# A hybrid Hyena and attention layer on one core: an early skip row, a first stage by channel pairs, and zeros multiplied ahead of it

## The chip, the cores and the metric

The kernel runs on one core of a Trainium2 chip. The core has a matmul engine (PE, TensorE), a vector engine (DVE), a scalar engine (ACT), GpSimd (POOL) and a sync engine (SP), each with an instruction queue of its own that is worked off in order. SP, ACT and POOL issue transfers, which share 16 DMA engines. The metric is the device time of one execution in microseconds.

## The reference

One layer of a bidirectional encoder, for 1024 positions of width 1024, all in float32:

```python
h = rms_norm(x, norm_g)
proj = h @ w_in                       # 1024 x 1024 by 1024 x 3328
hy_in, g_h, q, k, v, g_a = split(proj)
u = centred_short_conv(hy_in, conv_w, conv_b)        # 3 taps
hv, hx1, hx2 = split(u)
filt = hyena_filters(...)             # small sine MLP on positions, times a decay
k_f = two_sided_spectrum(filt)        # two orders, 512 channels
z = hx1 * long_conv(hv, k_f[:, 0], hyena_bias[0])    # y + u * bias
z = hx2 * long_conv(z, k_f[:, 1], hyena_bias[1])
y_a = windowed_sink_attention(rope(rms_norm(q)), rope(rms_norm(k)), v, sink)
y = concat(rms_norm(z) * silu(g_h), rms_norm(y_a) * silu(g_a))
out = x + y @ w_out
```

## The kernel before

**Arithmetic.** Large products run on PE in float32r, a rounded form. Each factor is split into a high part and the rest (`h[:, 0]` and `h[:, 1]` for x, `w_hi` and `w_lo` for a weight), and three matmuls are summed: high by high, high by rest, rest by high. ACT writes the high parts (`x_high`, a copy or a product with the norm's gain), DVE the rests (`x_low`, `lo_part`).

**The prelude** (`prelude`) comes first. x lies transposed, in two halves of 512 positions (h = 0 and 1) with 8 channel tiles k each. `load_x` queues on SP the transfers of x, two channel tiles at a time (512 KB), and among them the weights of the first two projection tiles (`raw[0]` in two pieces, `raw[1]` in one). The first two projections over half 0 (n = 0 and 1) are written out by hand as a list of (tile, low part or not, from k, to k); PE starts the second one only after six of the first one's eight channel tiles. Then come half 1 of both (`part(0, 1)`, `part(1, 1)`), the third projection, and between them x's squares and their sums (`x_square`, `x_add`, `x_sum`), from which the norm's factor is made (`rsqrt`, `x_rows`), and the filter's MLP (`next(mlp)`). `tables()` queues the loads of the DFT tables and of the first decay. `in_order` fixes the order of the prelude on each engine as it is written.

**The main part** is woven from two generators (`weave`): the Hyena branch, then attention, on one side; on the other the projections that are left, tile by tile, which fill PE. Behind the prelude the framework's scheduler sets the order on each engine, from the dependences, the priorities (`high_priority`) and its own estimates; so one edit can shift the order far behind it. The Hyena branch goes through eight units (order o, quarter s of the channels). In each, `filter_spectrum` makes the filter's values (`gen`), multiplies them by the decay (`eo`), adds a row of `hyena_bias` to the first row of `eo` (L626, the row `skip`), and transforms `eo` on PE (`dft`); `long_conv` then transforms u (`fw`), multiplies, and goes back (`inv`). The decay `dec` and the row `skip` of a unit are loaded on SP where `filter_spectrum` begins, but for the first decay. Each has one buffer.

**The output weights** (`wo`) are loaded while the last gate projections run: for the first half eight pieces of 256 KB through two buffers (`output_weights`, L1022 to L1029), so that a load waits until DVE has finished with the piece two before it. The first output products (`po`, L1115 to L1117) are filler for attention.

## Time and profile before

| | us |
|---|---|
| median of 3 runs (lowest to highest) | 648.45 (647.7 to 650.78) |
| the profiled execution | 647.31 |
| its span | 645.5 |
| PE busy | 624.0 (97%) |
| DVE busy | 530.9 (82%) |
| ACT busy | 267.2 (41%) |

The span leaves out 1.8 us of the profiled execution's time, and that execution is 1.1 us below the median. Busy time counts an engine as busy while any instruction of it is in flight. The time that PE sat idle is 645.5 - 624.0 = 21.5 us.

### The profile page before, as it was taken

Reading aid. Unit: us, or ns where it says so; the run is one execution under the profiler, and the core shown is the slowest. Engines: PE = TensorE matmul, PEld = TensorE weight load, DVE = VectorE, ACT = ScalarE, POOL = GpSimd, SP = SyncE. Lnnn points to the kernel's source line nnn. Section 1 sums busy time; section 2 is a strip of 40 time slices with the busy share of each in tenths; the row PEclk is TensorE's granted clock in tenths of the full one; section 3 lists DMA queues with packets and bytes.
Section 4 is the critical chain, followed back from the end, with each engine's and each line's share of the span. In section 5 each row is a group of like instructions: output and inputs, shape, how many; then the busy total and the mean of one; then the engine's idle time right before and its main releaser. Section 6 shows DMA issues by size and latency. Waiting matters only on the chain.

```text
span 645.5 us, 10611 instructions
## 1 busy us (share of the span) xinstructions
PE 624.0 (97%) x3958; PEld 552.6 (86%) x3958; DVE 530.9 (82%) x1187; ACT 267.2 (41%) x505; POOL 65.3 (10%) x83
## 2 busy tenths in 40 slices
PE   5999899999999999999999999999989999999997
PEld 4888898988999889899998898778877888889885
DVE  6959379899799997988999979589997888876431
ACT  6756424325541355441432241445463454444210
POOL 0121102112110131220111101100110000000000
PEclk9999999999999999999999999999996999999999
DMA  8956936767852689684287735733642324313321
GB/s 330 288 129 149 289 87 165 188 141 166 243 119 83 179 205 220 155 184 119 64 207 192 195 99 149 219 115 121 204 150 99 113 83 136 133 34 115 100 76 55
DMA packets 46964, 98.37 MB, mean 152 GB/s; under 512 B 6713, under 2 KB 15425, under 8 KB 46657
## 3 DMA queue, kind: packets, MB, share of 16 engines
q1 hardware_dynamic: 32640, 63.79, 29.9%
q0 software_dynamic: 10720, 26.21, 21.3%
q10 hardware_dynamic: 3552, 7.71, 3.3%
q8 instruction: 31, 0.51, 0.3%
q14 instruction: 21, 0.16, 0.1%
HBM read 53.65 MB, written 22.02 MB: 117 GB/s over the span
## 4 chain that ended last, share of the span: by engine, by line
PE 74%; DVE 13%; DMA 6%; issue 4%; ACT 2%; SPq 0%; POOL 0%; ACTq 0%; POOLq 0%; DVEq 0%
PE dft L636 7%; PE proj L255 7%; PE proj L257 7%; PE proj L256 7%; PE pv L991 5%; PE fw L752 4%; PE po L1116 4%; PE po L1117 4%; PE po L1115 4%; PE inv L793 4%; PE qkv L501 3%; PE qkv L500 3%; PE qkv L499 3%; PE smax L931 2%; DMA woraw<-in_w_out 2%
## 5 line engine op out<-in xcount | busy, mean ns | idle before, releaser
L255 PE MATMUL proj<-h,w_hi 128*128 128x512 f32 x304 | 121.8, 401 | 0.0
L257 PE MATMUL proj<-h,w_lo 128*128 128x512 f32 x304 | 120.0, 395 | 0.0
L256 PE MATMUL proj<-h,w_hi 128*128 128x512 f32 x304 | 119.8, 394 | 0.0
L223 POOL DMA_DIRECT2D w_lo<-wraw x48 | 43.1, 927 | 244.1 <-ACT w_lo L222 223.4
L255 PEld LDWEIGHTS proj<-h,w_hi 128*128 128x128 f32 x304 | 57.2, 188 | 11.1 <-issue 0.7
L256 PEld LDWEIGHTS proj<-h,w_hi 128*128 128x128 f32 x304 | 57.2, 188 | 11.1 <-issue 0.7
L257 PEld LDWEIGHTS proj<-h,w_lo 128*128 128x128 f32 x304 | 57.2, 188 | 10.9
L220 ACT CAST w_hi<-wraw 128x512 fp32r<-128x512 f32 x48 | 29.4, 619 | 70.8 <-PE proj L256 49.0
L500 PE MATMUL qkv<-w_lo,h 128*128 128x256 f32 x192 | 54.7, 285 | 0.0
L501 PE MATMUL qkv<-w_hi,h 128*128 128x256 f32 x192 | 54.6, 284 | 0.0
L499 PE MATMUL qkv<-w_hi,h 128*128 128x256 f32 x192 | 54.6, 284 | 0.0
L991 PEld LDWEIGHTS pv<-vv,pf 128*128 128x128 f32 x352 | 46.5, 199 | 3.5 <-issue 1.4
L991 PE MATMUL pv<-vv,pf 128*128 128x66 f32 x352 | 47.1, 278 | 1.4 <-DVE ao L996 1.3
L636 PE MATMUL dft<-eo,d 128*128 128x128 f32 x352 | 45.4, 276 | 1.7 <-DVE eo L626 1.7
L636 PEld LDWEIGHTS dft<-eo,d 128*128 128x128 f32 x352 | 42.6, 192 | 2.5 <-DVE eo L626 1.9
L500 PEld LDWEIGHTS qkv<-w_lo,h 128*128 128x128 f32 x192 | 36.8, 191 | 0.1
L499 PEld LDWEIGHTS qkv<-w_hi,h 128*128 128x128 f32 x192 | 36.7, 191 | 0.1
L501 PEld LDWEIGHTS qkv<-w_hi,h 128*128 128x128 f32 x192 | 36.8, 191 | 0.0
L936 DVE CUSTOM_DVE_ANT_0 mj<-smax,mask 128x384 f32<-128x384 f32 (+1 forms) x64 | 33.2, 519 | 2.2 <-PE smax L931 1.2
L793 PE MATMUL inv<-V,di 128*128 128x128 f32 x256 | 34.3, 275 | 0.0
L977 ACT ACTIVATE pf<-st 128x768 f32<-128x768 f32 (+1 forms) x32 | 24.2, 757 | 22.0 <-DVE st L974 21.1
L222 ACT ACTIVATE w_lo<-wraw 128x512 fp32r<-128x512 f32 x48 | 29.8, 628 | 8.4 <-PE qkv L500 8.3
(215 smaller groups left out, 1437.3 us busy)
## 6 DMA issues: line engine op xcount, KB each, us to landing
wraw<-in_w_in SPq DMA_DIRECT2D x48, 256.0 KB, 3.5
w_lo<-wraw POOLq DMA_DIRECT2D x48, 256.0 KB, 4.5
hy<-hsc ACTq DMA_DIRECT2D x12, 512.0 KB, 3.4
u<-hy SPq DMA_DIRECT2D x12, 512.0 KB, 3.7
hsc<-hs POOLq DMA_DIRECT2D x9, 511.5 KB, 5.5
hsc<-hraw POOLq DMA_DIRECT2D x9, 511.5 KB, 4.6
x<-in_x_t SPq DMA_DIRECT2D x8, 512.0 KB, 7.4
dec<-in_decay SPq DMA_DIRECT2D x8, 512.0 KB, 5.7
```

What stands on the lines that cost most here:

```text
L222: nc.scalar.mul(l, raw, -1.0)
L223: nc.gpsimd.dma_start(l.bitcast(F32), raw, accum_op=ALU.add)
L255: nc.tensor.matmul(pt, hi[:, k], xh, start=k == 0, stop=False)
L256: nc.tensor.matmul(pt, hi[:, k], xl, start=False, stop=False)
L257: i = nc.tensor.matmul(pt, lo[:, k], xh, start=False, stop=k == 7)
L499: nc.tensor.matmul(pt[:, b], hh, hi[:, :, k], start=k == 0, stop=False)
L500: nc.tensor.matmul(pt[:, b], hh, lo[:, :, k], start=False, stop=False)
L501: i = nc.tensor.matmul(pt[:, b], hl, hi[:, :, k], start=False, stop=k == 7)
L636: nc.tensor.matmul(out, m, eo[:, t, e], start=n == 0, stop=n == len(terms) - 1)
L793: nc.tensor.matmul(pt[:, k], self.di[:, t + k, c], v[:, t + k, c], start=c == 0, stop=c == 1)
L936: V.tensor_tensor_reduce(out=junk[:, 0:nk], in0=pm[:, 0:nk], in1=mask, op0=ALU.add, op1=ALU.max, scale=1.0, scalar=NEG, accum_out=mx[:, 4 ...
L991: nc.tensor.matmul(pv[:, h], probs[:, n, cols], self.vv[:, k0 + n, g], start=n == 0, stop=n == nk - 1)
```

## The change

Four edits go together.

1. **First stage by pairs.** The list written by hand gives way to a loop: for each pair of x's channel tiles, both projections' high parts, then both projections' low parts. Both weights are loaded in halves, the first halves behind x's first pair, the second halves behind x's third pair, and the order of the work on ACT and DVE follows. Over half 1, `part(0, 1)` and `part(1, 1)` advance in turn, two channel tiles at a time.
2. **Zeros.** A corner of the tile `row`, 128x128, is set to zero, and PE multiplies it by itself 18 times (`WARM`) into a spare bank ahead of the first projection.
3. **First skip row.** It is loaded in `tables()`, behind the first decay (`skip0`).
4. **Later skip rows and decays.** Both loads get the priority of u's loads (`2 * HP`), and the skip row moves to the pool of the decay.

```diff
--- before.py
+++ after.py
@@ -40,6 +40,8 @@
 
 FIRST = 3
 HP = 200
+
+WARM = 18
 RT = math.sqrt(0.5)
 TWO_PI_A = 6.28125
 TWO_PI_B = 2.0 * math.pi - 6.28125
@@ -120,6 +122,8 @@
         nc, a = self.nc, self.a
         pk = cp.tile([P, 192], F32, name="consts")
         nc.scalar.dma_start(pk, a["consts"])
+        self.row = cp.tile([P, 2, 512], F32, name="row")
+        nc.vector.memset(self.row[:, 0, 0:P], 0.0)
         self.ones = cp.tile([P, 1], F32, name="ones")
         nc.vector.memset(self.ones, 1.0)
         nc.scalar.activation(self.ones, self.ones, AF.Sin)
@@ -130,7 +134,6 @@
         self.identr = cp.tile([P, P], F32R, name="identr")
 
         self.rstd = cp.tile([P, 8], F32, name="rstd")
-        self.row = cp.tile([P, 2, 512], F32, name="row")
         self.zssq = cp.tile([P, 4, 8], F32, name="zssq")
 
 
@@ -142,10 +145,9 @@
         for h in range(2):
             for k in range(0, 8, 2):
                 q.dma_start(self.xt[h][:, k : k + 2], a["x_t"][h][:, k : k + 2])
-                if h == 0 and k < 4:
-                    q.dma_start(raw[0][:, 2 * k : 2 * k + 4], a["w_in"][ct[0]][:, 2 * k : 2 * k + 4])
-            if h == 0:
-                q.dma_start(raw[1], a["w_in"][ct[1]])
+                if h == 0 and k in (0, 4):
+                    for n in range(2):
+                        q.dma_start(raw[n][:, k : k + 4], a["w_in"][ct[n]][:, k : k + 4])
         return self.weight_load(ct[2])
 
     def x_high(self, h, k, e):
@@ -291,22 +293,26 @@
         del self.order[:2]
         w = [self.first_slot() for _ in range(2)]
 
+        idle = ps.tile([P, P], F32, tag="g", name=self.nm("idle"))
+        for _ in range(WARM):
+            nc.tensor.matmul(idle, self.row[:, 0, 0:P], self.row[:, 0, 0:P], start=True, stop=True)
+
+
         def lo_part(n, c):
             hi, lo = (x[:, 0, c] for x in w[n])
             V.tensor_tensor(out=lo, in0=raw[n][:, c], in1=hi.bitcast(F32), op=ALU.subtract)
 
         for k in range(0, 8, 2):
             self.x_high(0, k, A)
-            if k < 4:
-                half = slice(2 * k, 2 * k + 4)
-                A.copy(w[0][0][:, 0, half], raw[0][:, half])
             self.x_high(0, k + 1, V if k in (0, 4) else A)
+            if k in (0, 4):
+                for n in range(2):
+                    A.copy(w[n][0][:, 0, k : k + 4], raw[n][:, k : k + 4])
             self.x_low(0, k)
             self.x_low(0, k + 1)
-            if k < 4:
-                lo_part(0, half)
-        A.copy(w[1][0][:, 0], raw[1])
-        lo_part(1, slice(0, 8))
+            if k in (0, 4):
+                for n in range(2):
+                    lo_part(n, slice(k, k + 4))
         raws = [sp.tile([P, S], F32, tag=t, name=self.nm("hraw")) for t in ("raw", "raw", "t2")]
         banks = {}
 
@@ -336,12 +342,11 @@
                 nc.tensor.matmul(banks[n, 0], hi, xh, start=k == 0, stop=False)
                 nc.tensor.matmul(banks[n, 0], hi, xl, start=False, stop=False)
 
-        for n, low, k0, k1 in (
-            (0, 0, 0, 2), (0, 1, 0, 2), (0, 0, 2, 4), (0, 1, 2, 4), (0, 0, 4, 6), (0, 1, 4, 6), (1, 0, 0, 4),
-            (0, 0, 6, 8), (0, 1, 6, 8), (1, 0, 4, 8), (1, 1, 0, 8),
-        ):
-            for k in range(k0, k1):
-                first(n, k, low)
+        for k in range(0, 8, 2):
+            for low in range(2):
+                for n in range(2):
+                    for i in range(k, k + 2):
+                        first(n, i, low)
 
         for k in range(0, 8, 2):
             self.x_high(1, k, A)
@@ -354,12 +359,16 @@
             self.x_square(1, k)
             self.x_add(0, (k + 2) % 8)
         tables()
-        all_of(part(0, 1))
-        next(mlp)
+        c0, c1 = part(0, 1), part(1, 1)
+        for n in range(4):
+            next(c0), next(c1)
+            if n == 1:
+                next(mlp)
         for k in (2, 4, 6, 0):
             self.x_add(1, k)
         next(mlp)
-        all_of(part(1, 1))
+        all_of(c0)
+        all_of(c1)
         self.ahead.append(self.weights(*self.order.pop(0)))
         ss = ps.tile([P, 8, 2], F32, tag="g", name=self.nm("xss"))
         self.x_sum(0, ss)
@@ -601,13 +610,13 @@
         nc = self.nc
         V = nc.vector
         ADD, SUB = ALU.add, ALU.subtract
-        if (o, s) == (0, 0):
-            dec = self.dec0
-        else:
+        dec, skip = self.dec0, self.skip0
+        if (o, s) != (0, 0):
             dec = self.dp.tile([P, 8, CH], F32, tag="dec", name=self.nm("dec"), bufs=1)
-            nc.sync.dma_start(dec, self.a["decay"][s])
-        skip = fp.tile([1, CH], F32, tag="skip", name=self.nm("skip"), bufs=1)
-        nc.sync.dma_start(skip, self.a["hyena_bias"][0:1, o, s * CH : (s + 1) * CH])
+            skip = self.dp.tile([1, CH], F32, tag="skip", name=self.nm("skip"), bufs=1)
+            with self.tc.high_priority(2 * HP):
+                nc.sync.dma_start(dec, self.a["decay"][s])
+                nc.sync.dma_start(skip, self.a["hyena_bias"][0:1, o, s * CH : (s + 1) * CH])
         eo = fp.tile([P, 8, 2, CH], F32, tag="eo", name=self.nm("eo"), bufs=1)
         wf = self.wf[:, o, s].rearrange("p e c -> p (e c)")
         for t in range(0, 8, 2):
@@ -1217,6 +1226,7 @@
                     xp = pool(py, "x", 1, side="right")
                     self.dp = dpool
                     self.dec0 = dpool.tile([P, 8, CH], F32, tag="dec", name="dec0")
+                    self.skip0 = dpool.tile([1, CH], F32, tag="skip", name="skip0")
                     mlp = self.filter_mlp(mp, keep, ps)
                     w0, w1 = (self.filter_weights(o, fw, keep, ps) for o in range(2))
                     start = len(nc.cur_bb.bb.instructions)
@@ -1228,6 +1238,7 @@
                     def tables():
                         nc.sync.dma_start(self.d, a["dft"])
                         nc.sync.dma_start(self.dec0, a["decay"][0])
+                        nc.sync.dma_start(self.skip0, a["hyena_bias"][0:1, 0, 0:CH])
                         nc.sync.dma_start(self.dn, a["dft_neg"])
                         next(w0)
```

The start of PE's queue, before and then after. `proj_188` and `proj_212` are the first projection's bank, `proj_189` and `proj_213` the second's; `idle` is the spare bank.

```order
L336 MATMUL proj_188<-h_89,w_hi 128x512
L337 MATMUL proj_188<-h_89,w_hi 128x512
L336 MATMUL proj_188<-h_89,w_hi 128x512
L337 MATMUL proj_188<-h_89,w_hi 128x512
L334 MATMUL proj_188<-h_89,w_lo 128x512 x2
L336 MATMUL proj_188<-h_89,w_hi 128x512
L337 MATMUL proj_188<-h_89,w_hi 128x512
L336 MATMUL proj_188<-h_89,w_hi 128x512
L337 MATMUL proj_188<-h_89,w_hi 128x512
L334 MATMUL proj_188<-h_89,w_lo 128x512 x2
L336 MATMUL proj_188<-h_89,w_hi 128x512
```

```order
L298 MATMUL idle_166<-row 128x128 x18
L342 MATMUL proj_212<-h_89,w_hi 128x512
L343 MATMUL proj_212<-h_89,w_hi 128x512
L342 MATMUL proj_212<-h_89,w_hi 128x512
L343 MATMUL proj_212<-h_89,w_hi 128x512
L342 MATMUL proj_213<-h_89,w_hi 128x512
L343 MATMUL proj_213<-h_89,w_hi 128x512
L342 MATMUL proj_213<-h_89,w_hi 128x512
L343 MATMUL proj_213<-h_89,w_hi 128x512
L340 MATMUL proj_212<-h_89,w_lo 128x512 x2
L340 MATMUL proj_213<-h_89,w_lo 128x512 x2
```

The zeros stand ahead, and the second projection joins at the first pair of channel tiles rather than behind the sixth tile.

SP's queue around the Hyena branch's first unit: first before, from the loads of u's first tiles on; then after, the prelude's tables and the loads around those of u.

```order
L808 DMA u_606<-hy_63 128x1024
L808 DMA u_736<-hy_67 128x1024
L818 DMA di<-in_dft_inv 128x2048
L610 DMA skip_524<-in_hyena_bias 1x128
L608 DMA dec_781<-in_decay 128x1024
L207 DMA wraw_1487<-in_w_in 128x512
L610 DMA skip_783<-in_hyena_bias 1x128
L808 DMA u_919<-hy_71 128x1024
```

```order
L556 DMA mlp_in<-in_mlp_in 128x904
L1239 DMA d<-in_dft 128x2048
L1240 DMA dec_128<-in_decay 128x1024
L1241 DMA skip_129<-in_hyena_bias 1x128
L1242 DMA dn<-in_dft_neg 128x768
L599 DMA w_13_300<-in_filt_w 64x1024
```

```order
L209 DMA wraw_1510<-in_w_in 128x512
L817 DMA u_629<-hy_63 128x1024
L817 DMA u_759<-hy_67 128x1024
L618 DMA dec_804<-in_decay 128x1024
L619 DMA skip_805<-in_hyena_bias 1x128
L827 DMA di<-in_dft_inv 128x2048
L817 DMA u_942<-hy_71 128x1024
```

The first skip row has gone up to the prelude, ahead of `dn`; behind the loads of u come the second unit's decay and skip row, and the table `di` has gone behind both.

PE's queue where the output products begin, before and then after. `po` is an output bank, `st` the attention scores of a pair of heads, `pv` its values, `bT` transposed queries, `proj` the last projection.

```order
L256 MATMUL proj_4729<-h_90,w_hi 128x512
L257 MATMUL proj_4729<-h_90,w_lo 128x512
L991 MATMUL pv_4746<-vv,pf_4684 128x66
L951 MATMUL bT_4691<-identr,qq_4080 66x128 x4
L951 MATMUL bT_4698<-identr,qq_4080 66x128 x4
L991 MATMUL pv_4746<-vv,pf_4684 128x66 x5
L1115 MATMUL po_4983<-wo_4443,yh 128x512
L1116 MATMUL po_4983<-wo_4443,yh 128x512
L1117 MATMUL po_4983<-wo_4443,yl 128x512
L969 MATMUL st_4736<-qb_4696,kt_3918 128x256
L968 MATMUL st_4736<-qa_4586,kt_3917 128x256
L969 MATMUL st_4736<-qb_4696,kt_3918 128x256
```

```order
L977 MATMUL st_4872<-qa_4616,kt_3940 128x256
L978 MATMUL st_4872<-qb_4726,kt_3941 128x256
L977 MATMUL st_4872<-qa_4616,kt_3940 128x256
L978 MATMUL st_4872<-qb_4726,kt_3941 128x256
L977 MATMUL st_4872<-qa_4616,kt_3940 128x256
L978 MATMUL st_4872<-qb_4726,kt_3941 128x256
L258 MATMUL proj_4752<-h_90,w_hi 128x512
L259 MATMUL proj_4752<-h_90,w_lo 128x512
L1124 MATMUL po_5006<-wo_4466,yh 128x512
L1125 MATMUL po_5006<-wo_4466,yh 128x512
L1126 MATMUL po_5006<-wo_4466,yl 128x512
L1124 MATMUL po_5006<-wo_4466,yh 128x512
```

Before, 20 of attention's matmuls `st` from `qb` stand ahead of the first `po`, and the last projection is finished well ahead of it; after, 29 stand ahead of it and the last projection ends right in front of it.

## The prediction

> **What bounds the kernel now.** I read the page's busy times first, then a table of stretches, then the order of time at the places that the change touches.

> ```profile
> span 645.5 us, 10611 instructions
> PE 624.0 (97%) x3958; PEld 552.6 (86%) x3958; DVE 530.9 (82%) x1187; ACT 267.2 (41%) x505; POOL 65.3 (10%) x83
> ```

> PE is in use for 624.0 of 645.5 us. A change can gain only what PE sits idle, 21.5 us, and what PE runs slowly. The stretches, with the busy time and the count of each engine (first column: length):

> ```profile
> core 0: us, PE busy (x) PEld busy (x) DVE busy (x) ACT busy (x) POOL busy (x), PEclk, DMA share, GB/s
> 0.00:6.96 6.96, 0.00 (x0) 0.00 (x0) 1.20 (x5) 2.92 (x5) 1.16 (x5) 1.00 0.68 219
> 6.96:12.68 5.72, 5.72 (x14) 4.49 (x15) 5.33 (x10) 4.53 (x7) 0.00 (x0) 1.00 1.03 416
> 12.68:20.49 7.81, 7.81 (x36) 6.44 (x35) 7.81 (x13) 7.58 (x11) 0.00 (x0) 1.00 1.04 415
> 68.70:78.30 9.60, 7.86 (x67) 7.66 (x65) 1.60 (x4) 3.13 (x5) 1.75 (x2) 1.00 0.97 317
> 480.00:500.00 20.00, 16.66 (x80) 14.05 (x80) 15.52 (x43) 7.09 (x14) 0.54 (x1) 0.74 0.41 139
> ```

> Three places stand out: 6.96 us before the first matmul, then 14 matmuls in 5.72 us where the next 36 take 7.81; 1.74 us of PE idle at 68.7 to 78.3; and a stretch near 484 us with a low clock. The start in order of time:

> ```profile
> 6.96 0.79 PE L336 MATMUL proj<-h,w_hi 128*128 128x512 f32 x1 [6.96 <-ACT w_hi L302]
> 10.54 0.63 PE L336 MATMUL proj<-h,w_hi 128*128 128x512 f32 x1
> 13.89 0.39 PE L336 MATMUL proj<-h,w_hi 128*128 128x512 f32 x1
> 18.90 1.98 PE L334 MATMUL proj<-h,w_lo 128*128 128x512 f32 x8
> 20.71 0.39 PE L255 MATMUL proj<-h,w_hi 128*128 128x512 f32 x1
> ```

> A matmul of the same shape takes 0.63 us at 10.54 and 0.39 at 13.89, and by the table 14 of them begin in 5.72 us and 36 in the next 7.81, with no wait between: PE starts at about half speed and changes near 12.7 us, after 5.7 us of work. (The column PEclk shows 1.00 there; the spacing decides.) The eight low products, 18.90 to 20.71, show the full pace: 0.226 us each.

> **The change part by part.**

> *Zeros.* They need only the cleared tile. DVE's first instruction now starts at 0.82 us, so I take 1.1 us for PE's first zero product. The nearest rows for the price are the same 128x128 float32 product, eight of them as 16 records, up to the next matmul:

> ```profile
> 0.82 0.06 DVE L124 MEMSET ones<- 128x1 f32 x1 [0.82 <-PEq L1473]
> ...
> 39.29 1.95 PE L187 MATMUL xr<-consts,rsy 128*128 128x128 f32 x16
> 40.99 0.47 PE L255 MATMUL proj<-h,w_hi 128*128 128x512 f32 x1
> ```

> 1.70 / 8 = 0.2125 us each at the full pace, 0.425 at half. If 5.7 us of work bring the clock here too, it is there at 6.8 us: 5.7 / 0.425 = 13.4 zeros slow, 4.6 x 0.2125 = 1.0 us quick, end at 7.8. The first projections then start 0.8 us later than now, but 48 x 0.226 = 10.9 us later they are done: 18.7 in place of 20.5, 1.8 us gained. Bounds: if zeros don't bring the clock at all, they end at 1.1 + 7.65 = 8.75, 14 real matmuls are slow (5.7 us), 34 quick (7.7 us), end at 22.15, a loss of 1.65. If the clock comes early enough that zeros end by 6.96, the gain is 2.65.

> *By pairs.* PE needs a pair every 12 x 0.226 = 2.7 us: at 7.8, 10.5, 13.2 and 15.9. The transfers run at 415 GB/s by the table, so what stands ahead of x's second and third pair, 256 KB more, costs 0.6 us, and ahead of the fourth, 512 KB more, 1.3 us. Rows on ACT that waited for these pairs:

> ```profile
> 7.56 0.72 ACT L157 ACTIVATE h<-x,consts 128x512 fp32r<-128x512 f32 x1 [0.65 <-DMA x<-in_x_t]
> 10.79 1.34 ACT L157 ACTIVATE h<-x,consts 128x512 fp32r<-128x512 f32 x2 [0.56 <-DMA x<-in_x_t]
> ```

> So the second pair is there at 8.2 and the fourth at 12.1, against 10.5 and 15.9: over 2 us each for ACT (0.7 us a tile) and DVE. No wait; half 1 comes as before, since the bytes ahead of it are the same. DVE's work is the same but for four low parts of 512 columns, 4 x 0.69, in place of 2 x 0.69 + 1.22: 0.15 us more.

> *What is late next.* The sums of squares on PE need DVE's additions:

> ```profile
> 21.84 4.54 DVE L173 TENSOR_TENSOR x<-x 128x1024 f32<-128x1024 f32 x4
> 26.37 4.60 DVE L173 TENSOR_TENSOR x<-x 128x1024 f32<-128x1024 f32 x4
> 32.48 1.84 PE L177 MATMUL xss<-ones,x 128*128 128x1 f32 x16
> ```

> DVE works without a pause there and is done at 30.97, with the 0.15 us and a little more about 31.2. PE would come at 32.48 - 1.8 = 30.7 and waits until 31.2. Of 1.8 us, 1.25 are left; even the 2.65 would be cut to that. I take 1.25, and -1.65 to 1.5 as bounds. The two projections over half 1, in turn, need each pair of half 1 later than before, so nothing new waits there; reordering them costs no work.

> *First skip row.* The chain of waits holds a transfer here, and the table of waits shows what it cost PE:

> ```profile
> 68.72 9.15 DMA skip<-in_hyena_bias
> ```

> ```profile
> PE dft L636 <- DVE eo L626: 1.7, 1, 1.7
> ```

> The order of time on DVE, and on SP's queue:

> ```profile
> 67.35 2.48 DVE L620 TENSOR_TENSOR eo<-gen,dec 128x512 f32<-128x512 f32 x4
> 69.75 0.27 DVE L625 TENSOR_TENSOR eo<-eo 1x128 f32<-1x128 f32 x1
> 77.96 0.28 DVE L626 SCALAR_TENSOR_TENSOR eo<-eo,skip 1x128 f32<-1x128 f32 x1 [7.95 <-DMA skip<-in_hyena_bias]
> ```

> ```profile
> 67.34 0.81 SPq L808 DMA_DIRECT2D u<-hy  x2
> 68.20 0.46 SPq L818 DMA_DIRECT2D di<-in_dft_inv  x1
> 68.72 0.46 SPq L610 DMA_DIRECT2D skip<-in_hyena_bias  x1
> ```

> 512 bytes took 9.15 us, behind 2 MB of u and `di`; DVE sat 7.95 us, PE only 1.74, because 64 matmuls of `qkv` stood in between. With the row loaded in the prelude, at about 14 us, it is there long before. The gain is PE's 1.74 us at most, not DVE's eight. Nothing else takes its place by the rows: in the new order 11 `qkv` matmuls, 0.12 us each, lie between the last `gen` and the first `dft`, 1.3 us, while DVE needs about 1.1 us after that `gen` (69.83 - 68.7) and 0.3 for the skip row. Bounds 0 (another wait of the same length) and 1.74; I take 1.7. The extra load in the prelude is one issue of 0.33 us on SP ahead of `dn`, whose first reader is `dft`, 50 us later: nothing.

> *Later rows and decays raised.* No other wait for them is in the trace, so there is nothing to gain directly. They go up in SP's queue and wait there for their one buffer, as a skip row did once already; SP holds what is behind them meanwhile. The second row is the first reader of `di`:

> ```profile
> SPq L610 <- DVE eo L626: 14.1, 1, 14.1
> ```

> ```profile
> 116.87 0.91 PE inv L793 x8
> ```

> Behind the second unit's pair come `di`, u, a store and then weights. In the first unit DVE frees both buffers by about 70 us (69.75 + 0.27), over 40 us before `di` is read. I take zero. The wait of 14.1 us cost PE nothing in the trace; as the outer bound I keep a loss of 1.7 us, a stop like that of the first skip row, if one of the seven pairs reaches a weight tile.

> *What the shift does later.* The Hyena branch now runs up to eight microseconds ahead of the projections that fill PE. PE is at 100% up to 400 us, so nothing shows there. It shows near the first output products, here on PE, ACT and DVE in order of time and as a stretch:

> ```profile
> 481.51 0.50 PE L1115 MATMUL po<-wo,yh 128*128 128x512 f32 x1 [0.87 <-ACT wo L1028]
> 482.22 0.39 PE L968 MATMUL st<-qa,kt 128*128 128x256 f32 x1 [0.21 <-ACT pf L977]
> 484.84 0.80 PE L1115 MATMUL po<-wo,yh 128*128 128x512 f32 x1 [1.64 <-ACT wo L1028]
> ```

> ```profile
> 484.17 0.62 ACT L1028 CAST wo<-woraw 128x512 fp32r<-128x512 f32 x1 [2.00 <-DMA woraw<-in_w_out]
> 487.02 0.62 ACT L1028 CAST wo<-woraw 128x512 fp32r<-128x512 f32 x1 [1.52 <-DMA woraw<-in_w_out]
> ```

> ```profile
> 489.06 0.82 DVE L882 TENSOR_TENSOR qkv<-qkv,rm 128x640 f32<-128x640 f32 x1
> ```

> ```profile
> 484.00:494.00 10.00, 9.16 (x36) 8.28 (x37) 7.58 (x18) 3.34 (x7) 0.25 (x1) 0.50 0.14 52
> ```

> PE waits 0.87 + 0.21 + 1.64 = 2.7 us within 5 us for pieces of the output weights, and then runs at half clock (0.50) for most of ten microseconds; I count 9.2 us, the busy time, half of which is 4.6 us more. Whole price 7.3 us. The new order begins `po` three attention units later against the pieces (29 `st` from `qb` ahead of it, not 20), which helps; but `kT` and `aT` of block 4 now stand between the `po`, and these need DVE's rotation, which was done only at 489.9. I take no difference, and keep 7.3 us either way as the bounds.

> The sum against the execution's own time: 647.3 - 1.25 - 1.7 = 644.35. The median of the runs is 1.1 us above that execution, so 645.4.

> **The rivals.**

> *The cold stretch goes.* Everything above and, near 484 us, no half clock: 4.6 us less, of which DVE's rotation lets PE use perhaps 3 to 4, so 645.4 - 4 = 641.5. For it speaks that six of eight pieces are cast ahead of `po` (three before); against it the new place of `kT`. [...]

> *The start gains nothing.* Zeros don't count for the clock, or PE waits again behind the sums: -1.65 to 0 at the start, 1.7 from the skip row. 645.4 + 1.25 + 1.0 = about 648, no change. Against it: the clock rose at 12.7 us with nothing but work having gone before.

> *Slower: a second cold stretch.* The shifted order near 484 us makes PE wait both for the last pieces of `wo` and, after it, for `kT` of block 4. From the point where the waits in 5 us reach again some 2.7 us, a second 7.3 us is due: 645.4 + 7.3 = 652.7. For it: DVE has both the rotation and the low parts of `wo` queued there. Against it: one longer wait by itself left the clock alone, this one at about 415 us:

> ```profile
> PE kT L908 <- ACT kt L909: 1.4, 1, 1.4
> ```

> **How the numbers follow.** The forecast 645.4 has 0.42, the stretch that goes 0.28, no gain at the start 0.17, a second stretch 0.13. 0.5% of 648.45 is 3.2 us, about what a measurement of this kernel can tell from no change; its bounds are 645.2 and 651.7. The forecast lies on the first bound, a bit under half of it faster (0.19); with 0.28 that is 0.47. The rest of it (0.23) and most of the third case (0.15) are the same: 0.38. The second stretch and a rest of the third case: 0.15. The range reaches down to the second case with its full 7.3 us less a little, 639, and up to 651.5, which leaves out most of the last case. The forecast's own range is 643.5 to 647.5.

> **What the changed profile would show.** Matmul starts 0.23 us apart from the first projection on, the first one at 7 to 8.5 us, the low products of the stage done at about 18.7. PE waiting half a microsecond before the sums. L635 (the skip row's addition) without a wait for a DMA and the first `dft` near 70 us. Near 480 us, waits of PE for `wo` or `kT` and the clock behind them. Wrong would be: spacing of 0.43 us after the zeros; a new wait of PE for `w_hi` between 85 and 400 us, which would mean that SP was held up; two stretches of low clock.

## The result, and the profile after

The changed kernel takes 652.47 us (median of 7 runs, 650.86 to 654.77) against 648.45: a ratio of 1.0061, 95% interval 1.0036 to 1.0086. It is slower by 4 us, where 3 us of gain were forecast. Its profiled execution took 652.58 us, 1.8 of them outside the span, as before. Of the runs further down, one slow execution of `start_alone` (1241.51 us) and one of `before_order_start_alone` (653.39) are left out of the ratios but not of the medians, and without the first the median of `start_alone` is 654.46.

The page of the changed kernel, its span, PE's busy time and PE's granted clock in 40 slices:

```profile
span 650.8 us, 10698 instructions
...
PE 630.2 (97%) x3994; PEld 557.6 (86%) x3994; DVE 532.3 (82%) x1189; ACT 268.3 (41%) x506; POOL 65.4 (10%) x83
...
PEclk9999999998999999989999999999998999999999
```

and the granted clock before:

```profile
PEclk9999999999999999999999999999996999999999
```

PE is busy for 6.2 us more, and 6.1 of these are the zeros, which stand where it sat idle. So its idle time should have fallen to about 15 us; it is 650.8 - 630.2 = 20.6. And the clock dips at three places, in slices 10, 18 and 31; before, at one, in slice 31.

The start, PE in order of time, the sums of squares, and the first transposes behind the prelude:

```profile
1.06 6.08 PE L298 MATMUL idle<-row 128*128 128x128 f32 x36 [1.06 <-DVE ones L128]
18.72 0.39 PE L257 MATMUL proj<-h,w_hi 128*128 128x512 f32 x1
30.49 1.84 PE L179 MATMUL xss<-ones,x 128*128 128x1 f32 x16
51.02 1.13 PE L434 MATMUL uT<-consts,hsc 128*128 128x128 f32 x8
```

The next projection begins at 18.72, against 20.71 before: 2.0 us gained. At the sums (32.48 before) all of it is still there. The first transposes come 1.5 us sooner (52.55 before), but here PE has two more projection products behind it by then (161 since 18.72, against 159 since 20.71; 0.45 us), so nothing of the 2.0 is lost. The first skip row no longer keeps DVE or PE (its addition, the first transform, and the next wait of PE):

```profile
67.89 0.27 DVE L635 SCALAR_TENSOR_TENSOR eo<-eo,skip 1x128 f32<-1x128 f32 x1
68.52 2.39 PE L645 MATMUL dft<-eo,d 128*128 128x128 f32 x20
75.56 1.13 PE L761 MATMUL fw<-u,d 128*128 128x128 f32 x8 [0.63 <-DMA u<-hy]
```

So by 80 us the kernel was some 3 us ahead (2.0 and 1.74 - 0.63 = 1.1), where 1.25 + 1.7 were forecast: the sum came out because the two terms were off in opposite ways, which is luck. Then PE's waits, summed (total, times, longest):

```profile
PE uT L434 <- DMA hsc<-hraw: 8.9, 2, 5.4
PE smax L940 <- DVE mx L945: 3.1, 5, 1.2
```

and the same transposes before:

```profile
PE uT L425 <- DMA hsc<-hraw: 0.3, 1, 0.3
```

`smax` waited 3.7 us in all, with one wait for `den`; before, 0.6. The stretches around the two waits (length, PE, its weight loads, DVE, ACT and POOL busy, granted clock, DMA share, GB/s):

```profile
141.40:144.80 3.40, 1.26 (x6) 0.72 (x4) 3.40 (x6) 2.31 (x2) 1.78 (x2) 1.00 0.77 130
144.80:148.20 3.40, 0.14 (x1) 0.17 (x2) 3.40 (x10) 0.00 (x0) 0.00 (x0) 0.50 1.04 237
148.20:151.60 3.40, 3.40 (x13) 3.01 (x14) 0.10 (x1) 1.07 (x2) 0.00 (x0) 0.50 0.75 177
277.90:281.30 3.40, 0.02 (x1) 0.05 (x1) 3.15 (x10) 2.95 (x4) 1.84 (x3) 1.00 1.03 189
281.30:284.70 3.40, 3.40 (x16) 3.40 (x17) 0.16 (x1) 0.00 (x0) 0.77 (x1) 0.50 1.08 196
```

PE stops at 142.7, the clock halves at 144.8, and when the data land PE works another 3.4 us at half pace; at 277.7 likewise. A third stretch (499.8 to 506.6) follows the waits of `smax`. In the working part of the three, 13 us, half is lost: 6.5 us, against 4.6 before. The account, by waits and clock: -2.0 (start), -1.1 (skip row, 1.74 less the new 0.63), +8.6 (transposes), +1.9 (half clock); near the first output products -2.7 (`wo`, gone), +3.1 (`smax`), -1.9 (`kT`), -1.3 (`pv`). That is +4.6 of the 5.3 us by which the spans differ.

**Why the transposes wait.** The short convolution of a Hyena tile (`short_conv`) goes through four engines behind the tile's last projection: DVE scales the second half into `hraw` (L270), ACT makes the middle tap `hsc` (L412) and the side taps (L422, L423), and POOL adds these to `hsc` by two transfers in series (L425). Then PE transposes (`uT`, L434). This is tile s = 1 of the second projection, the changed kernel, all engines in order of time, from the last product of its projection on:

```profile
124.36 0.39 PE L259 MATMUL proj<-h,w_lo 128*128 128x512 f32 x1
...
131.91 0.69 DVE L270 TENSOR_TENSOR hraw<-proj,row 128x512 f32<-128x512 f32 x1
...
133.26 1.24 ACT L412 ACTIVATE hsc<-hraw,consts 128x1024 f32<-128x1024 f32 x1
...
135.90 0.86 POOL L425 DMA_DIRECT2D hsc<-hs  x1 [8.96 <-ACT hs L422]
...
142.27 0.39 PE L257 MATMUL proj<-h,w_hi 128*128 128x512 f32 x1
142.48 0.86 POOL L425 DMA_DIRECT2D hsc<-hraw  x1 [3.11 <-DVE ism L790]
...
148.06 1.94 PE L434 MATMUL uT<-consts,hsc 128*128 128x128 f32 x8 [5.40 <-DMA hsc<-hraw]
```

and the same tile before:

```profile
111.85 0.39 PE L257 MATMUL proj<-h,w_lo 128*128 128x512 f32 x1
...
118.97 0.68 DVE L268 TENSOR_TENSOR hraw<-proj,row 128x512 f32<-128x512 f32 x1
...
126.78 0.86 POOL L416 DMA_DIRECT2D hsc<-hs  x1 [11.94 <-ACT hs L413]
...
133.78 0.86 POOL L416 DMA_DIRECT2D hsc<-hraw  x1 [6.14 <-DMA hsc<-hs]
...
143.93 1.04 PE L425 MATMUL uT<-consts,hsc 128*128 128x128 f32 x8
```

From `hraw` to the transposes it takes 15.5 us after (131.91 + 0.69 to 148.06), 12.2 of them for the two transfers in series (135.90 to 142.48 to 148.06). (The page puts POOL's wait at 142.48 down to DVE. The first transfer was over no sooner than that result: ACT, which waits for it too, goes on at 141.79.) DVE came to `hraw` 7 us after PE had finished with the tile, being at Hyena work, but it did so before as well (112.1 to 118.97). Nor was the chain as a whole shorter before: from 112.1 to about 138.4 (133.78 and the 4.6 us that the page gives as the median of such a transfer), 26 us; after, from 124.6 to 148.06, 23.5 us. What changed is PE's row. Between a tile's last projection product and its first transpose stand (products counted in the built order; us from the two traces, with the wait of the tile's own transposes taken off):

| | before | changed |
|---|---|---|
| second projection, s = 1 | 148: 72 `proj`, 16 `inv`, 16 `gen`, 28 `dft`, 16 `fw`; 31.9 us | 79, all `proj`; 18.1 us, waits 5.40 |
| third projection, s = 1 | 88; 18.8 us, waits 0.3 | 156; 34.9 us |
| first projection, s = 3 | 148; 31.5 us | 80: 72 `proj`, 8 `uT`; 17.4 us, waits 3.55 |
| the six others, least | 148; 32.0 us | 148; 32.1 us |

The planner put the Hyena branch's transforms ahead of the tile's last product, or behind its transposes, and not between. PE works in order, so the distance in its row is the time that the taps get: 18.1 and 17.4 us, where 23.5 and 21.0 were needed. How much is needed differs from tile to tile and run to run: 18.8 us fell short by 0.3 us before and by 1.5 in before_order_skip_row_alone (below), 19.2 by 3.9 in start_alone.

### The profile page after: what moved, and what is told of

Read it like the earlier page. It is cut to its first block, busy times and chain, and to the rows that moved or that the text cites. A ratio compares the mean times of both kernels' runs of the same rounds, so it can differ in the third digit from the quotient of the medians.

```text
span 650.8 us, 10698 instructions
## 1 busy us (share of the span) xinstructions
PE 630.2 (97%) x3994; PEld 557.6 (86%) x3994; DVE 532.3 (82%) x1189; ACT 268.3 (41%) x506; POOL 65.4 (10%) x83
## 4 chain that ended last, share of the span: by engine, by line
PE 73%; issue 11%; DMA 8%; DVE 6%; ACT 2%; POOL 1%; ACTq 0%; POOLq 0%
PE proj L258 8%; PE proj L259 8%; PE proj L257 8%; PE dft L645 5%; PE pv L1000 5%; PE po L1124 4%; PE po L1126 4%; PE po L1125 4%; PE inv L802 4%; PE fw L761 3%; PE qkv L508 2%; PE qkv L510 2%; PE qkv L509 2%; PE st L977 2%; PE st L978 2%
## 5 line engine op out<-in xcount | busy, mean ns | idle before, releaser
L258 PEld LDWEIGHTS proj<-h,w_hi 128*128 128x128 f32 x304 | 57.5, 189 | 10.9 <-issue 0.7
L1000 PEld LDWEIGHTS pv<-vv,pf 128*128 128x128 f32 x352 | 45.0, 191 | 1.2
L1000 PE MATMUL pv<-vv,pf 128*128 128x66 f32 x352 | 45.0, 269 | 0.0
L802 PE MATMUL inv<-V,di 128*128 128x128 f32 x256 | 35.8, 279 | 0.0
L802 PEld LDWEIGHTS inv<-V,di 128*128 128x128 f32 x256 | 33.4, 196 | 0.8 <-issue 0.2
```

The costliest lines, as they stand in the source:

```text
L258: nc.tensor.matmul(pt, hi[:, k], xl, start=False, stop=False)
L802: nc.tensor.matmul(pt[:, k], self.di[:, t + k, c], v[:, t + k, c], start=c == 0, stop=c == 1)
L1000: nc.tensor.matmul(pv[:, h], probs[:, n, cols], self.vv[:, k0 + n, g], start=n == 0, stop=n == nk - 1)
```

## The experiments

Behind the prelude the written program is the same before and after (4833 instructions, and the one load of the first skip row). So the order itself can be carried over. A table of numbers (`PINNED`) names each engine's instructions in the wanted row, and each is made to follow the one ahead of it, without a semaphore:

```diff
-        Kernel(tc, aps, out).run()
+        k = Kernel(tc, aps, out); k.run(); pin(k)
...
+        for a, b in zip(row, row[1:]):
+            k.tc.add_manual_dep(b, a.name, k.NOSYNC, reason="pinned")
```

Held in its own order in this way, a kernel is the same program as without the table. All times, with the ratio to the kernel before on the same chip (its medians there: 649.0 to 649.8), the profiled span, the transposes' wait for their taps and the time at half clock ahead of the last outputs (by the record of the granted clock):

| run | median us | ratio, 95% | span | `uT` waits | half clock |
|---|---|---|---|---|---|
| before | 648.45 | | 645.5 | 0.3 | 10.2 |
| changed | 652.47 | 1.0061 (1.0036 to 1.0086) | 650.8 | 8.9 | 17.1 |
| after_in_befores_order | 640.57 | 0.9877 (0.9853 to 0.9901) | 637.3 | 0 | 0 |
| before_in_afters_order | 653.44 | 1.0069 (1.0047 to 1.009) | 654.7 | 8.0 | 13.7 |
| start_alone | 655.94 | 1.0111 (1.0082 to 1.014) | 652.7 | 3.9 | 13.7 |
| skip_rows_alone | 648.25 | 0.9993 (0.9978 to 1.0007) | 647.2 | 5.5 | 10.2 |
| transposes_later | 644.96 | 0.9945 (0.9927 to 0.9964) | 643.0 | 0 | 3.4 |
| changed_transposes_one_half_later | 639.53 | 0.9861 (0.9829 to 0.9894) | 637.0 | 0 | 3.4 |
| before_order_skip_row_alone | 645.61 | 0.9961 (0.9934 to 0.9988) | 643.4 | 1.5 | 10.2 |
| before_order_start_alone | 645.46 | 0.9947 (0.9921 to 0.9974) | 642.3 | 0 | 6.8 |
| before_transposes_one_half_later | 652.67 | 1.0058 (1.0039 to 1.0077) | 650.7 | 0.2 | 20.5 |
| repaired_without_zeros | 640.53 | 0.9862 (0.9843 to 0.9882) | 639.1 | 0 | 3.4 |
| repaired_without_pairs | 641.06 | 0.9883 (0.9863 to 0.9904) | 637.2 | 0 | 0 |
| waits_filled_with_zeros | 648.44 | 0.9985 (0.9968 to 1.0001) | 647.2 | 0 (filled) | 6.8 |

**The orders crossed.** First the changed kernel in the order of the kernel before:

> The changed kernel with every engine's instructions behind the prelude held in the order that they had in the kernel before (a table of numbers; only the first skip row's load is gone from it, and the later loads stand where they stood before, so their raising is undone). Theory 'order' (the early edits gain what was forecast, and the loss is the new order behind the prelude, in which the transposes of the short convolution wait for its taps): 647.3 - 1.5 to 1.8 - 1.7 = 644 us (643 to 645.5), transposes waiting 0.5 us or less, one stretch of half clock near 484. Rival 'ahead' (work that comes 3 us earlier collides with transfers whatever its order): 651 to 653, with the waits of the changed kernel or others in their place. Rival 'start lost' (zeros and pairs gain nothing in the end): 646 to 648.

Then the start of the kernel before in the order of the changed one:

> The reverse: the first stage of the kernel before (no zeros, by whole tiles, the two late projections one after the other), with the first skip row in the prelude, and behind the prelude every engine in the order of the changed kernel. Theory 'order': the waits of the transposes are there again (about 9 us in all or a little less, as everything around them moves by the same 1.5 us) with two or three stretches of half clock, 652.5 + 1.5 to 1.8 = 654 us (652.5 to 656). Rival 'ahead': the start is late again, so no collision, 646 to 648.5. Rival 'start lost': 652.5.

The first was 8 us faster than before, more than any theory said; the second is as slow as the changed kernel. Same order, nearly the same waits: the loss belongs to the order behind the prelude (SP's row, with the raised loads, is part of it), not to the edits of the start and the first skip row. The first one's granted clock on its page, its wait for the pieces of `wo`, and the stretch in which the cold clock had been:

```profile
PEclk9999999999999999999999999999999999999999
```

```profile
PE po L1124 <- ACT wo L1037: 1.6, 2, 0.8
```

```profile
480.00:500.00 20.00, 18.27 (x113) 15.21 (x114) 17.82 (x55) 8.75 (x20) 0.00 (x0) 1.00 0.43 139
```

The Hyena branch and attention come 2.5 us (at 141 us) to 4 us (at 480) sooner, PE's waits for the pieces of `wo` shrink to 0.8 us apiece, six microseconds apart, and the clock holds (1.00 where it was 0.74): the 4.6 us of the old cold stretch and 1.1 us of its waits go too. Of the start's 2.0 us a wait of 0.9 for the filter's MLP takes part here: 1.1 + 1.7 + 4.6 + 1.1 = 8.5, measured 8.2 between the spans. This is the profiled execution, one of the two fastest of six (639.06 us, mean granted clock 1.0). In the other four the clock averaged 0.991 to 0.995, at 640.5 to 643.2 us, so it still dipped somewhere; and one of 17 executions of the kernel before kept it (1.0, 645.47 us). The cold stretch is thus a matter of odds, and its whole 4.6 us are not in the medians. In the second, against the 2 or 3 stretches expected, four came.

**Each half of the change by itself, ordered by the planner.** The edits of the start, the changed kernel without those of the skip rows and decays:

```diff
-        dec, skip = self.dec0, self.skip0
-        if (o, s) != (0, 0):
+        if (o, s) == (0, 0):
+            dec = self.dec0
+        else:
 ...
-            with self.tc.high_priority(2 * HP):
 ...
-                        nc.sync.dma_start(self.skip0, a["hyena_bias"][0:1, 0, 0:CH])
```

> Zeros, pairs and the two late projections in turn, without the edits of the skip rows and decays; the order behind the prelude is the planner's own. Theory 'order': 647.3 - 1.5 = 645.8 if its order lets the transposes wait no more than before, and each 1 us of their wait with the half clock behind it comes on top (a reshuffle like the changed kernel's gives 652 to 654). Rival 'raised loads do it': 645 to 646 with no such wait, since nothing is raised. Rival 'start lost': 647 to 648.5.

and the other half, the same lines put into the kernel before (signs turned round):

> The first skip row in the prelude and the later rows and decays raised, on the first stage of the kernel before. Theory 'order': 647.3 - 1.7 = 645.6 if its order keeps the transposes' wait at 0.3 us, 650 to 653 if it is reshuffled like the changed kernel's. Rival 'raised loads do it': 651 to 655 with waits behind a load that SP holds. Rival 'no gain from the row': 647 to 648.5.

Each gets an order of its own with new waits for the taps, so neither half is to blame by itself, and the raised loads are not needed for the loss: nothing is raised in the slowest of all, which is above the 652 to 654 that were expected for a reshuffle. The other half took 648.25 us, between the two figures of 'order' and in the range of the rival 'no gain from the row'; but in its trace the first `dft` no longer waits, and 5.5 us of waits for the taps have come. start_alone also shows what the first skip row can cost (PE waiting for it, and the stretch behind):

```profile
78.08 4.29 PE L645 MATMUL dft<-eo,d 128*128 128x128 f32 x20 [5.23 <-DVE eo L635]
```

```profile
75.00:82.00 7.00, 3.92 (x19) 3.92 (x20) 1.04 (x3) 0.58 (x1) 0.86 (x1) 0.51 1.04 355
```

5.23 us, where before it was 1.74, with the half clock behind it.

**The two waits alone.** Only PE's row is touched:

```diff
 MATMUL proj_1810<-h_90,w_hi 128x512
-MATMUL uT_1615<-consts,hsc_1502 128x128 x4
-MATMUL uT_1620<-consts,hsc_1502 128x128 x4
 ...
 MATMUL inv_967<-V_948,di 128x128
+MATMUL uT_1615<-consts,hsc_1502 128x128 x4
+MATMUL uT_1620<-consts,hsc_1502 128x128 x4
```

> The changed kernel in its own order, held by a table, with one thing moved on PE: the two groups of eight transposes that waited for their taps (at 148 and 281 us) stand 36 and 24 matmuls later. All other engines keep their rows. Theory 'order' in its narrow form (these two waits and the half clock that begins in them are the loss): both waits go, 8.9 us, and two of the three stretches of half clock, about 1.75 us each as PE worked some 3.5 us in each; 652.6 - 8.9 - 3.5 = 640 us (639 to 643, if the inverse products that now come first wait a little for DVE). The third stretch near 500 us stays or moves. Rival 'other places': Hyena work behind the transposes was late too, so another wait takes their place, 648 to 652.

Both waits and both half-clock stretches are gone, by moving 16 transposes. But 7.5 us came of the 12.4 expected. PE's next waits say where the rest is:

```profile
145.72 0.91 PE L802 MATMUL inv<-V,di 128*128 128x128 f32 x6 [0.61 <-DVE V L734]
160.69 1.38 PE L645 MATMUL dft<-eo,d 128*128 128x128 f32 x10 [1.69 <-ACT fc L670]
164.54 1.76 PE L761 MATMUL fw<-u,d 128*128 128x128 f32 x11 [0.93 <-ACT fc L670]
```

The Hyena work behind the transposes was short of DVE and ACT results by 3.2 us here (0.44 more at 275 us): part of what the rival 'other places' said.

**A repair that leaves the order to the planner.** The transposes are released half a projection later:

```diff
-LATE = 0
+LATE = 1
```

> The changed kernel with LATE = 1: the transposes are released behind the second half of the next tile, not the first, and the planner orders everything anew. In its order the least PE work between a tile's last projection and its transposes is 27 us, against 17.9 in the changed kernel. Theory 'order': no wait of the transposes, 652.6 - 8.9 - 3.5 = 640 (639 to 644; the stretch near 500 may come or go with 3 us). Rival 'other places': 648 to 652, since what reads the transposed tiles now comes later and the Hyena branch waits for u.

639.5, as forecast and the lowest median of all (its interval overlaps that of the crossed order). No wait of the transposes is left; the page and the largest wait:

```profile
span 637.0 us, 10699 instructions
...
PEclk9999999999999999999999999999998999999999
```

```profile
PE st L977 <- ACT pf L986: 1.5, 2, 1.1
```

The same number in the kernel before:

> The kernel before with LATE = 1 alone, ordered anew by the planner; least PE work between a tile's last projection and its transposes 23 us (before 18.9). Its transposes hardly waited (0.3 us), so by the theory 'order' there is little to gain: 647.3, less up to 4.6 if the cold stretch near 484 goes, plus up to 3.5 for new waits: 643 to 651. The rival, that the later transposes themselves are the whole gain of the repaired kernel (639.5) and the edits of the start and the skip row give nothing: 639 to 641.

It is 3.8 us slower than before by the ratio, a little above the range expected. The transposes wait 0.2 us, but the first `dft` now waits 3.97 us for the skip row, and the clock is at half for 6.8 us behind it and for 13.7 us near 490. So the later transposes are not a gain by themselves; with the edits they free 13 us.

**The halves in the order of the kernel before.** Both pinned by its table; the skip row without the raising, which the table undoes:

```diff
+                        nc.sync.dma_start(self.skip0, a["hyena_bias"][0:1, 0, 0:CH])
 ...
-        if (o, s) == (0, 0):
-            dec = self.dec0
-        else:
+        dec, skip = self.dec0, self.skip0
+        if (o, s) != (0, 0):
 ...
```

> The kernel before, in its own order on every engine, with one edit: the first skip row's load stands in the prelude. If the edits' gains add up: 647.3 - 1.7 = 645.6, with the cold stretch near 484 as before; if being 1.7 us ahead is enough to end that stretch, 641. 647 to 649 if the row's gain is given back later.

> The kernel before, in its own order behind the prelude, with the edits of the start alone (zeros, pairs, late projections in turn). The first skip row still stands behind u and di on SP, whose issue does not come earlier than their buffers allow, so PE, 1.5 us ahead, should wait 1.5 us longer for it: 647.3 - 0 = 646 to 648. If the gain stands: 645.8, or 641 if the cold stretch near 484 ends too.

By ratio the row brings 0.39%, the start 0.53%, both together 1.23%: about additive within the intervals. By the spans 2.1 and 3.2 us. The row's term was about right (1.7), and the old cold stretch stayed, as expected at 1.7 us ahead. Of the start I expected nothing here, a miss: its wait for the row grew, but from 1.74 to 2.26 us only, and the half clock shrank from 10.2 to 6.8.

**Zeros or pairs.** On the repaired kernel, in its order, `WARM` at 0, and the first stage's loads, casts and list of products as before:

```diff
-WARM = 18
+WARM = 0
```

> The changed kernel with LATE = 1 (639.5 us), every engine held in that kernel's order, with WARM = 0: no zeros. As the prediction had it, the first 14 real products run at half pace again and the low products of the stage end near 20.5 in place of 18.7: 639.5 + 1.8 less what the sums' wait takes = 640.8 to 641.5. If zeros are worth nothing in the end: 639.5. If a late start also shifts the later order into a wait or a cold stretch: up to 645.

```diff
-        for k in range(0, 8, 2):
-            for low in range(2):
-                for n in range(2):
-                    for i in range(k, k + 2):
-                        first(n, i, low)
+        for n, low, k0, k1 in (
+            (0, 0, 0, 2), (0, 1, 0, 2), (0, 0, 2, 4), (0, 1, 2, 4), (0, 0, 4, 6), (0, 1, 4, 6), (1, 0, 0, 4),
 ...
```

> The same kernel and order with the zeros kept, but loads, casts and products of the first stage as in the kernel before (one weight tile's products first, the second's weights behind all of x's first half). At full pace PE then asks for x's pairs every 1.4 to 2 us while they land every 2 us or so, the fourth at 12.1 plus its cast: it should wait 1 to 2 us in the stage, 640.5 to 641.5. If the pairs don't matter: 639.5.

The end of the first stage, without zeros and then without pairs (PE in order of time):

```profile
20.94 0.39 PE L257 MATMUL proj<-h,w_hi 128*128 128x512 f32 x1
```

```profile
12.71 0.50 PE L345 MATMUL proj<-h,w_hi 128*128 128x512 f32 x1 [0.47 <-DVE h L163]
...
20.99 0.39 PE L258 MATMUL proj<-h,w_hi 128*128 128x512 f32 x1
```

20.94 and 20.99, where both edits give 18.48 in this order and neither gave 20.71: each is worth nothing at this place without the other. Without zeros the products start 0.43 us apart up to 12.8 us and 0.23 after it; without pairs PE, now quick, waits for x's parts, 1.0 us in all (and its first real product came at 7.76, not 7.22, as the zeros took 6.95 us, not 6.40: 0.5 us that are not the pairs'). Of the 2.5 us only 1.0 and 1.5 show in the medians, and the intervals of the three ratios overlap: the price at the end is not resolved. (In the profiled execution without pairs no half clock came near 490 us, which hides some 1.7 us, half of the 3.4 us at half clock in the repaired kernel.)

**Waits kept, idleness taken away.**

```diff
                 pt = ps.tile([P, 4, P], F32, tag="g", name=self.nm("uT"))
+                for _ in range({(1, 1): 24, (0, 3): 16}.get((n, s), 0) * (h == 0)):
+                    nc.tensor.matmul(pt[:, 0, :], self.row[:, 0, 0:P], self.row[:, 0, 0:P], start=True, stop=True)
```

> The changed kernel in its own order, held by a table, with 24 and 16 products of 128x128 ahead of the two groups of transposes that wait (148 and 281 us), into the bank that the transposes then write: 24 x 0.2125 = 5.1 and 16 x 0.2125 = 3.4 us of PE work in waits of 5.40 and 3.55 us. The transposes come no sooner. If idle time on PE is what halves the clock: no half clock at 145 to 152 and 281 to 285, 652.5 - 1.75 - 1.7 = 649 us (648 to 650.5), the waits' 8.9 us still paid. If something else halves it (the waiting itself, the transfers): the same stretches, 652 to 653.

The transposes come no sooner, and the clock stays (rows of PE, then of the same stretches as above):

```profile
143.25 5.52 PE L434 MATMUL uT<-row 128*128 128x128 f32 x48
148.66 1.13 PE L436 MATMUL uT<-consts,hsc 128*128 128x128 f32 x8
```

```profile
144.80:148.20 3.40, 3.40 (x33) 3.40 (x32) 3.40 (x10) 0.00 (x0) 0.05 (x1) 1.00 1.07 231
148.20:151.60 3.40, 3.40 (x23) 3.00 (x22) 0.86 (x3) 1.77 (x4) 0.00 (x0) 1.00 0.91 212
```

648.4 us against 649 expected. The price of the two waits is thus parted: 8.9 us of waiting, and about 4 of clock behind them (4.0 between the medians, 3.6 between the spans, 4.9 by the two ratios).

## Why the prediction was wrong

- **Zeros and pairs: right.** First zeros at 1.06 (forecast 1.1), nearly the full pace of 0.226 us after them (48 products from 7.44 to 18.72, 0.235 us each), stage done at 18.7 (18.7). PE waited once in it, 0.30 us for the first weights at 7.44.
- **What is late next: wrong, in the kernel's favour.** PE was to wait at the sums until DVE's last additions, at 31.2, which would leave 1.25 us. It came at 30.49 and worked through; the additions ended at 31.04, so only the last of the sixteen products can have needed them. All 2.0 us were left.
- **First skip row: right, less a term left out.** PE's 1.74 us went, the first `dft` at 68.5; a new wait of 0.63 for u took a third of it. In other orders the same row cost 4.0 and 5.2 us with half clock behind: in this case the early load is also an insurance.
- **Raised loads: taken as zero, not tried alone.** In the order of the kernel before they stand where they stood, and the time (640.6) is near that of the repaired kernel, where they are raised (639.5), in another order. Their own price stays open.
- **The step that failed: "What the shift does later".** It said "PE is at 100% up to 400 us, so nothing shows there", and priced only the place near 484 us. A full PE says that no wait was there in the old order; it does not say by how much each one was missed. The taps of the tightest tile had 18.8 us of PE work as cover and waited 0.3. The planner's new order gave that tile more cover, and took it from two others, which had 31.9 and 31.5 us and were left with 18.1 and 17.4: 8.9 us of waits and a good 3 us of half clock. The prediction's own sign of being wrong, two stretches of low clock, was met: there were three.
- **The size of the slow rival (652.7) was met by luck; its place and cause were not right.** It was written for `wo` and `kT` near 484 us. There the waits for `wo` went, as the first rival had it, and those of `smax` brought a stretch of their own. Where nothing else was in the way (order of the kernel before, or LATE = 1), a time near that first rival's 641.5 came: 640.6 and 639.5.
- **The idle time ahead of half clock: less than was thought.** A second stretch was forecast from some 2.7 us of waits within 5 us on. In before_in_afters_order one wait of 1.96 us was followed by half clock (last section).

## What to carry to other kernels

Where a scheduler orders the work, an edit is judged by two numbers: what it does, and what the new order does. They can be parted by holding the old order fixed; here it turned +0.6% into -1.2%. For each chain over several engines that ends on the bounding engine, count the work that stands between its start and its end in that engine's row, in both orders: a cover that shrinks below the chain's length is a stall, though the old profile shows hardly a wait. Here PE paid again in clock for waits of 5.40 and 3.55 us, and for one of 1.96 (next section). Filling the first two with idle products, where the waits themselves stayed, brought 4 us.

## What the runs showed of the hardware

```profile
73.50:76.90 3.40, 3.40 (x33) 3.40 (x32) 0.00 (x0) 0.58 (x1) 0.00 (x0) 1.00 0.95 225
76.90:80.30 3.40, 1.45 (x13) 1.28 (x12) 3.25 (x6) 0.00 (x0) 0.00 (x0) 1.00 1.03 343
80.40:83.80 3.40, 3.40 (x19) 3.40 (x18) 1.09 (x3) 1.29 (x3) 0.86 (x1) 0.50 0.84 340
```

In the changed kernel half clock followed the steps from 141.4, 277.9 and 496.4 us, with 2.13, 3.36 and 2.02 us idle. With less it came or did not: 1.70 us in the kernel before at 480 us brought it, 1.41 us at 412 us left the clock alone. Nor did a busy step always end it: in the kernel before, PE was busy throughout 487.2 to 490.7 us, and the half clock went on to 494.1. What decided there stays open.
